# Seven products in another order: the three without a weight sum first

## The chip, the cores and the metric

The kernel runs on one core of one Trainium2 chip. The metric is the device time of one execution in microseconds (us). The reference gives two layers of a decoder trunk for 256 tokens of width 2048, in float32; every large matrix is read from memory once per execution.

## The reference, cut to what matters

```python
for layer in range(2):
    h = rms_norm(x, norm_mix[layer])
    x = x + mixer[layer](h)                  # layer 0: window attention + SSD, layer 1: dilated attention
    h = rms_norm(x, norm_ffn[layer])
    u = jnp.einsum('bsd,df->bsf', h, w_up)   # (256, 2048) x (2048, 8192)
    x = x + jnp.einsum('bsf,fd->bsd', jnp.square(jax.nn.relu(u)), w_down)   # (256, 8192) x (8192, 2048)
```

The change touches the last of these products alone, in both layers: the squared activations times `w_down`.

## The kernel before, in words

**Precision.** Every float32 matrix is split into a high part (a rounded float32r copy, written by ScalarE, `whi`) and a low part (the rest, written by VectorE, `wlo`). A product is three matmuls on TensorE: high by high, high by low, low by high. So each 128x1024 piece of weights (two k-tiles of 128 rows, 512 columns) costs one ScalarE copy (`high`, L314), one VectorE subtraction (`low`, L324) and its matmuls.

**The plan.** All matmul work is one list, `plan`, of pieces; `run` (L291) goes through it. At piece i it issues, in this order, the low part of piece i+2, the load of piece i+6, the high part of piece i+3 and the weight sum of piece i+4 (L353 to L357). Then follow the evictions of the piece before (`pending`, L358), then some steps of the side work (`tick`, L171: transposes, squares, splits of activations), then the matmuls of piece i. Each engine works through its own queue in the order of issue, and semaphores make it wait for the others. There are five `whi` and four `wlo` buffers (L320, L327) and four for freshly loaded weights, `wraw` (L303): a low part can't be written before TensorE is done with the piece four places ahead of it, and a load of such weights waits for the low part that last read its buffer.

**Units and sevens.** An ordinary unit (`Unit`) is one stripe of 512 columns; its pieces have 12 matmuls each and accumulate in two banks (`acc`). `Seven` (L243) instead multiplies 256 tokens by a 1024x1024 block of `w_down` with seven block products in place of eight. It cuts the tokens, the rows and the columns of the block in two. Weights W11, W12, W21, W22 (rows, columns) and linear combinations of them meet activations or their combinations; products are added in PSUM banks (`sp`) and taken from there into the residual stream `res` by VectorE (`evict`, L281). A product is two pieces, h = 0 and 1, of six matmuls each. The raw weights lie in `sraw` tiles: SyncE loads 12 and 11 with product P1, 21 and 22 with P2 (`fetch`, L257). GpSimd adds W22 into tile 12 and then W12 into tile 11 by accumulating DMAs (`accumulate`, L271). Two more sums are made by VectorE (`add`, L265). In the order before:

| product | bank | weights | made from | evicted into (token half, stripe) |
|---|---|---|---|---|
| P1 | a | tile 11 | loaded | (0,0) |
| P2 | b | tile 21 | loaded | (0,0) |
| Q7 | c | tile 12 | accumulated by DMA | (1,1) |
| Q6 | a | tile t2 | 11 + 22, VectorE | (1,0) |
| Q5 | a | tile 11 | accumulated by DMA | (1,1) |
| Q4 | c | tile 21 | 21 + t2, VectorE | (1,0) |
| Q3 | a | tile 22 | loaded | (0,1) |

A bank is not cleared between its products: Q6 adds onto P1, Q5 onto both, and so on. So Q5's first matmul waits until VectorE has read Q6's state of bank a, and Q3's until it has read Q5's.

**Where the sevens stand.** The MLP (`mlp`, L951) has eight chunks c of 1024 hidden columns. In the plan, the products of chunk c stand among the up projections of the chunks after it (`mixed`, L1062): for c = 0 to 5 two sevens per chunk, one after the other, called the first and the second here, and one for c = 6; 13 per layer, 26 in all. For c = 0, 3 and 4, with 19 up pieces, the plan alternates one up piece and two pieces of *different* products, so that Q6's second piece and Q5's first stand side by side. For c = 1 and 2, with 18, it alternates one up piece and the two pieces of *one* product. For c = 5 the spacing is wider, and its second seven ends with six pieces in a row. The last, c = 6, has one piece between two others throughout. Before a chunk's first seven stand five up pieces, and the splits and sums of the next activations fall there.

Of the kernel before, what the change touches and what calls it, by code (L numbers as in the profile page):

```python
# [11 lines left out]
OP = mybir.AluOpType  # L12
# [28 lines left out]
def trunk(ctx: ExitStack, tc: tile.TileContext, x, norm_mix, norm_ffn, w_up, w_down, ab_w_in, ab_q_norm,  # L41
# [33 lines left out]
    V, S, PE = Engine(nc.vector, "V", 90, 1.04), Engine(nc.scalar, "S", 240, 0.83), Engine(nc.tensor, "PE", 0, 0.84)  # L75
# [157 lines left out]
    def unit(*a, **k):  # L233
# [1 line left out]

    SEVEN = (("P1", "a", "11"), ("P2", "b", "21"), ("Q7", "c", "12"), ("Q6", "a", "t2"), ("Q5", "a", "11"),
             ("Q4", "c", "21"), ("Q3", "a", "22"))
    LOADS = {"P1": ("12", "11"), "P2": ("21", "22")}  # L240
    SUMS = {"Q6": ("t2", "11", "22"), "Q4": ("21", "21", "t2")}

    class Seven:  # L243

# [12 lines left out]
        def fetch(self, p, h):  # L257
            for b in LOADS.get(SEVEN[p][0], ()):
                r, c = self.rows[int(b[0]) - 1] + h * KC, self.c0 + (int(b[1]) - 1) * W
                nc.sync.dma_start(self.tile(b, h),  # L260
                                  self.w[r * 128:(r + KC) * 128, c:c + W].rearrange("(k p) c -> p k c", p=128))
                if b == "12":
                    self.accumulate("12", 1, h)

        def add(self, p, h):  # L265
            if SEVEN[p][0] in SUMS:
                o, x, y = SUMS[SEVEN[p][0]]
                x, y = self.raw[x, h], self.raw[y, h]
                V.tensor_tensor(self.raw[o, h] if o != "t2" else self.tile(o, h), x, y, op=OP.add)

        def accumulate(self, b, half, h):  # L271

# [5 lines left out]
        def source(self, p, h):  # L278
            return self.raw[SEVEN[p][2], h]

        def evict(self, p):  # L281

            name, b, _ = SEVEN[p]
            t, j, op = {"P1": (0, 0, OP.add), "P2": (0, 0, OP.add), "Q6": (1, 0, OP.add), "Q7": (1, 1, OP.subtract),
                        "Q5": (1, 1, OP.subtract), "Q4": (1, 0, OP.add), "Q3": (0, 1, OP.subtract)}[name]
            r = self.to[t][j]
            V.tensor_tensor(r, r, self.bank[b], op=op)
            if p == 6 and self.after is not None:
                self.after()

    def run():  # L291
# [60 lines left out]
        for i, (u, c) in enumerate(todo):  # L352
            if i:  # L353
                low(i + AHEAD - 1)
                fetch(i + AHEAD - 1 + RAW)
                high(i + AHEAD)
                add(i + AHEAD + 1)  # L357
# [4 lines left out]
            if isinstance(u, Seven):  # L362
                p, h = c
                name, b, _ = SEVEN[p]
                if p in u.needs and h == 0:
# [836 lines left out]
```

## Time and profile before

| | |
|---|---|
| time, median of three runs | 2342.51 us (2342.3, 2342.51, 2350.98) |
| the profiled execution's own time | 2346.71 us |
| its span, first to last instruction | 2344.9 us |
| TensorE (PE) busy | 2275.7 us, 97% |
| VectorE (DVE) busy | 1771.5 us, 76% |
| ScalarE (ACT) busy | 1296.5 us, 55% |
| mean granted TensorE clock | 0.99 of full speed |
| DMA | 204 GB/s over the span |

The profile is of one execution. Its time is 1.8 us more than its span, and 4.2 us more than the median of the three runs. The sevens run from about 546 us on in layer 0 and from about 1677 to 2325 us in layer 1. A time stands for the whole kernel, but TensorE's idle time lies in a few places; what one of them is worth is read from a window around it.

### The profile page before, as it was taken

The numbers are of one execution on the slowest core, as the hardware profiler recorded it, in microseconds if no ns is written. First come the engines' busy times: TensorE is split into PE (matmuls) and PEld (weight loads), VectorE is DVE, ScalarE is ACT, GpSimd is POOL, SyncE is SP. The second block draws the span as 40 slices with busy tenths as digits, with TensorE's granted clock in tenths as the row PEclk, the third lists the DMA queues.
The fourth block names the chain that finished last, engine by engine and source line by source line (L and its number), as shares of the span: only waits on it lengthen the run. The fifth ranks groups of instructions, "written<-read, shape, count | busy, mean of one in ns | idle before, by whom it ended". The sixth has DMA issues, their size and how long they took to land.

```text
span 2344.9 us, 30293 instructions
## 1 busy us (share of the span) xinstructions
PE 2275.7 (97%) x11005; PEld 1878.8 (80%) x11005; DVE 1771.5 (76%) x2508; ACT 1296.5 (55%) x1627; POOL 133.7 (6%) x124
## 2 busy tenths in 40 slices
PE   8999999999999999999999999999999999999999
PEld 7999988887877878778788778778877877778777
DVE  6779886557877978778976767755687887878796
ACT  5565545445555656556665555554555555556563
POOL 1000000001100011101000000000101101011100
PEclk9999999999999999999999999999999999999999
DMA  7546555569687796978656555446869787696984
GB/s 229 163 136 195 182 175 185 188 186 298 167 256 207 207 288 183 262 206 251 193 172 188 160 155 176 155 161 188 261 172 286 198 241 229 184 295 172 266 229 133
DMA packets 257783, 479.29 MB, mean 204 GB/s; under 512 B 17317, under 2 KB 28113, under 8 KB 257633
## 3 DMA queue, kind: packets, MB, share of 16 engines
q1 hardware_dynamic: 219264, 416.34, 54.2%
q0 software_dynamic: 28800, 54.68, 13.0%
q10 hardware_dynamic: 9568, 6.34, 0.9%
q8 instruction: 86, 1.41, 0.2%
q14 instruction: 65, 0.52, 0.1%
HBM read 475.17 MB, written 2.13 MB: 204 GB/s over the span
## 4 chain that ended last, share of the span: by engine, by line
PE 81%; DMA 13%; DVE 4%; ACT 2%; issue 1%; SPq 0%; ACTq 0%; DVEq 0%
PE acc L71 58%; PE sp L71 17%; DMA wraw<-in_w_up_dram 11%; DVE wlo L71 2%; ACT whi L71 1%; PE uT L71 1%; PE sc L71 1%; PE o L71 1%; PE pT L71 1%; DVE sraw L71 1%; DVE res L71 1%; PE yp L71 1%; PE xT L71 1%; DMA sraw<-in_w_down_dram 1%; DMA wraw<-in_ab_w_in_dram 0%
## 5 line engine op out<-in xcount | busy, mean ns | idle before, releaser
L71 DVE TENSOR_TENSOR wlo<-wraw,whi 128x1024 fp32r<-128x1024 f32 (+1 forms) x584 | 706.6, 1215 | 268.9 <-PE acc L71 158.3
L71 ACT ACTIVATE whi<-wraw 128x1024 fp32r<-128x1024 f32 (+1 forms) x584 | 614.6, 1054 | 505.2 <-PE acc L71 295.3
L71 PE MATMUL acc<-whi,hThi 128*128 128x512 f32 (+1 forms) x1632 | 654.2, 401 | 10.7 <-ACT whi L71 8.5
L71 PE MATMUL acc<-wlo,hThi 128*128 128x512 f32 (+1 forms) x1632 | 641.0, 393 | 7.8 <-DVE wlo L71 7.8
L71 PE MATMUL acc<-whi,hTlo 128*128 128x512 f32 (+1 forms) x1632 | 639.2, 392 | 0.8 <-DVE hTlo L71 0.8
L71 ACT ACTIVATE whi<-sraw 128x1024 fp32r<-128x1024 f32 x364 | 383.6, 1059 | 351.8 <-DVE sraw L71 131.4
L71 DVE TENSOR_TENSOR wlo<-sraw,whi 128x1024 fp32r<-128x1024 f32 x364 | 443.7, 1222 | 131.2 <-ACT whi L71 50.6
L71 PEld LDWEIGHTS acc<-whi,hThi 128*128 128x128 f32 x1632 | 310.8, 190 | 78.7 <-ACT whi L71 10.8
L71 PEld LDWEIGHTS acc<-wlo,hThi 128*128 128x128 f32 x1632 | 310.9, 191 | 74.4 <-DVE wlo L71 14.0
L71 PEld LDWEIGHTS acc<-whi,hTlo 128*128 128x128 f32 x1632 | 310.3, 190 | 66.5 <-DVE hTlo L71 1.7
L274 POOL DMA_DIRECT2D sraw<-in_w_down_dram x104 | 125.3, 1211 | 2130.0 <-DMA sraw<-in_w_down_dram 760.0
L71 PE MATMUL sp<-whi,sh 128*128 128x512 f32 x416 | 164.0, 394 | 23.9 <-DVE res L71 23.9
L71 PE MATMUL sp<-wlo,sh 128*128 128x512 f32 x416 | 163.8, 394 | 0.3
L71 PE MATMUL sp<-whi,sl 128*128 128x512 f32 x416 | 163.8, 394 | 0.0
L71 DVE TENSOR_TENSOR res<-res,sp 128x512 f32<-128x512 f32 x182 | 124.6, 685 | 25.7 <-PE sp L71 25.1
L71 DVE TENSOR_TENSOR sraw<-sraw 128x1024 f32<-128x1024 f32 x104 | 126.9, 1220 | 0.0
L71 PEld LDWEIGHTS sp<-whi,sh 128*128 128x128 f32 x416 | 78.8, 189 | 45.5 <-ACT whi L71 24.7
L71 PE MATMUL acc<-hThi,whi 128*128 128x256 f32 x384 | 112.4, 293 | 0.0
L71 PE MATMUL acc<-hThi,wlo 128*128 128x256 f32 x384 | 108.6, 283 | 0.0
L71 PE MATMUL acc<-hTlo,whi 128*128 128x256 f32 x384 | 108.6, 283 | 0.0
L71 PEld LDWEIGHTS sp<-wlo,sh 128*128 128x128 f32 x416 | 78.6, 189 | 18.0 <-DVE wlo L71 2.2
L71 PEld LDWEIGHTS sp<-whi,sl 128*128 128x128 f32 x416 | 78.8, 189 | 16.4
(227 smaller groups left out, 2781.0 us busy)
## 6 DMA issues: line engine op xcount, KB each, us to landing
wraw<-in_w_up_dram SPq DMA_DIRECT2D x256, 512.0 KB, 5.0
sraw<-in_w_down_dram SPq DMA_DIRECT2D x208, 512.0 KB, 9.4
sraw<-in_w_down_dram POOLq DMA_DIRECT2D x104, 512.0 KB, 9.8
wraw<-in_ab_w_in_dram SPq DMA_DIRECT2D x96, 512.0 KB, 3.6
wraw<-in_c_w_qkv_dram SPq DMA_DIRECT2D x96, 512.0 KB, 4.1
wraw<-in_ab_w_out_dram SPq DMA_DIRECT2D x48, 512.0 KB, 3.5
wraw<-in_w_down_dram SPq DMA_DIRECT2D x48, 512.0 KB, 4.0
wraw<-in_c_w_o_dram SPq DMA_DIRECT2D x32, 512.0 KB, 3.5
```

The costliest lines, as they stand in the source:

```text
L71: return f(out, *a, **k)
L274: nc.gpsimd.dma_start(self.raw[b, h], self.w[r * 128:(r + KC) * 128, c:c + W].rearrange("(k p) c -> p k c", p=128), accum_op=OP.add)
```

## The change

The order of the seven products becomes P1, P2, Q3, Q7, Q6, Q5, Q4. Q3 gets a bank `d` of its own, which holds Q3 alone. Since bank a no longer passes through Q3, output (0,1) is made of two evictions: Q3's from d, and a second one of Q5's bank a. So VectorE has eight evictions per seven in place of seven, 26 more in all. The sum for Q6 is written over tile 22, which Q3 has used by then, and Q4 adds this tile; the tile t2 is no longer allocated (two per seven). The number of sums, of loads and of matmuls stays, and so does the order of the queues of SyncE, GpSimd and ScalarE.

```diff
@@ -235,10 +235,10 @@
 
 
 
-    SEVEN = (("P1", "a", "11"), ("P2", "b", "21"), ("Q7", "c", "12"), ("Q6", "a", "t2"), ("Q5", "a", "11"),
-             ("Q4", "c", "21"), ("Q3", "a", "22"))
+    SEVEN = (("P1", "a", "11"), ("P2", "b", "21"), ("Q3", "d", "22"), ("Q7", "c", "12"), ("Q6", "a", "22"),
+             ("Q5", "a", "11"), ("Q4", "c", "21"))
     LOADS = {"P1": ("12", "11"), "P2": ("21", "22")}
-    SUMS = {"Q6": ("t2", "11", "22"), "Q4": ("21", "21", "t2")}
+    SUMS = {"Q6": ("22", "11", "22"), "Q4": ("21", "21", "22")}
 
     class Seven:
 
@@ -266,7 +266,7 @@
             if SEVEN[p][0] in SUMS:
                 o, x, y = SUMS[SEVEN[p][0]]
                 x, y = self.raw[x, h], self.raw[y, h]
-                V.tensor_tensor(self.raw[o, h] if o != "t2" else self.tile(o, h), x, y, op=OP.add)
+                V.tensor_tensor(self.raw[o, h], x, y, op=OP.add)
 
         def accumulate(self, b, half, h):
 
@@ -281,10 +281,11 @@
         def evict(self, p):
 
             name, b, _ = SEVEN[p]
-            t, j, op = {"P1": (0, 0, OP.add), "P2": (0, 0, OP.add), "Q6": (1, 0, OP.add), "Q7": (1, 1, OP.subtract),
-                        "Q5": (1, 1, OP.subtract), "Q4": (1, 0, OP.add), "Q3": (0, 1, OP.subtract)}[name]
-            r = self.to[t][j]
-            V.tensor_tensor(r, r, self.bank[b], op=op)
+            for t, j, op in {"P1": ((0, 0, OP.add),), "P2": ((0, 0, OP.add),), "Q6": ((1, 0, OP.add),),
+                             "Q7": ((1, 1, OP.subtract),), "Q4": ((1, 0, OP.add),), "Q3": ((0, 1, OP.subtract),),
+                             "Q5": ((1, 1, OP.subtract), (0, 1, OP.subtract))}[name]:
+                r = self.to[t][j]
+                V.tensor_tensor(r, r, self.bank[b], op=op)
             if p == 6 and self.after is not None:
                 self.after()
```

**First place: VectorE's queue in the first seven of chunk 0, layer 0.** `wlo_...<-wraw` is the low part of an up piece, `wlo_...<-sraw` that of a seven's piece, `sraw<-sraw` a weight sum, `res<-res,sp` an eviction. Before, from the low part of the up piece behind the third product's first piece on:

```order
L71 TENSOR_TENSOR wlo_5443<-wraw_5379,whi_5429 128x1024
L71 TENSOR_TENSOR sraw_5447<-sraw_5220,sraw_5294 128x1024
L71 TENSOR_TENSOR wlo_5455<-sraw_5264,whi_5445 128x1024
L71 TENSOR_TENSOR res_82<-res_82,sp_5418 128x512
L71 TENSOR_TENSOR wlo_5467<-sraw_5447,whi_5457 128x1024
L71 TENSOR_TENSOR sraw_5473<-sraw_5267,sraw_5343 128x1024
L71 TENSOR_TENSOR wlo_5487<-wraw_5427,whi_5471 128x1024
L71 TENSOR_TENSOR wlo_5497<-sraw_5473,whi_5489 128x1024
L71 TENSOR_TENSOR res_82<-res_82,sp_5460 128x512
L71 TENSOR_TENSOR wlo_5508<-sraw_5220,whi_5499 128x1024
```

The same stretch in the changed kernel:

```order
L71 TENSOR_TENSOR wlo_5443<-wraw_5379,whi_5429 128x1024
L71 TENSOR_TENSOR wlo_5453<-sraw_5343,whi_5445 128x1024
L71 TENSOR_TENSOR res_82<-res_82,sp_5418 128x512
L71 TENSOR_TENSOR wlo_5465<-sraw_5217,whi_5455 128x1024
L71 TENSOR_TENSOR wlo_5483<-wraw_5427,whi_5469 128x1024
L71 TENSOR_TENSOR sraw_5294<-sraw_5220,sraw_5294 128x1024
L71 TENSOR_TENSOR wlo_5494<-sraw_5264,whi_5485 128x1024
L71 TENSOR_TENSOR res_82<-res_82,sp_5458 128x512
L71 TENSOR_TENSOR wlo_5506<-sraw_5294,whi_5496 128x1024
L71 TENSOR_TENSOR sraw_5343<-sraw_5267,sraw_5343 128x1024
L71 TENSOR_TENSOR wlo_5530<-wraw_5467,whi_5510 128x1024
L71 TENSOR_TENSOR wlo_5540<-sraw_5343,whi_5532 128x1024
```

The two sums for Q6 stand one product later, behind the low part of another up piece; a further eviction (Q3's, `sp_5458`) stands between; and `sraw_5294`, which is tile 22, takes the sum in place of the new tile `sraw_5447`.

**Second place: VectorE's queue at the end of the second seven of chunk 2.** Before, the low part of Q3's last piece, the eviction of Q4, the low parts of the first up pieces before the next chunk's sevens, and Q3's eviction:

```order
L71 TENSOR_TENSOR wlo_8180<-sraw_7917,whi_8172 128x1024
L71 TENSOR_TENSOR res_82<-res_82,sp_8015 128x512
L71 TENSOR_TENSOR wlo_8193<-wraw_8134,whi_8184 128x1024
L71 TENSOR_TENSOR wlo_8218<-wraw_8147,whi_8197 128x1024
L71 TENSOR_TENSOR wlo_8233<-wraw_8170,whi_8225 128x1024
L71 TENSOR_TENSOR res_82<-res_82,sp_7933 128x512
```

In the changed kernel:

```order
L71 TENSOR_TENSOR wlo_8179<-sraw_7915,whi_8171 128x1024
L71 TENSOR_TENSOR res_82<-res_82,sp_7933 128x512 x2
L71 TENSOR_TENSOR wlo_8193<-wraw_8132,whi_8183 128x1024
L71 TENSOR_TENSOR wlo_8218<-wraw_8145,whi_8197 128x1024
L71 TENSOR_TENSOR wlo_8233<-wraw_8169,whi_8225 128x1024
L71 TENSOR_TENSOR res_82<-res_82,sp_8054 128x512
```

Here the low part is that of Q4's last piece, the eviction of Q5 stands twice, and the low parts of the up pieces come behind both.

**Third place: VectorE's queue in the last six pieces of the second seven of chunk 5.** Before, from the eviction of Q6 on:

```order
L71 TENSOR_TENSOR res_82<-res_82,sp_9489 128x512
L71 TENSOR_TENSOR wlo_9664<-sraw_9419,whi_9648 128x1024
L71 TENSOR_TENSOR wlo_9676<-sraw_9460,whi_9668 128x1024
L71 TENSOR_TENSOR wlo_9688<-sraw_9421,whi_9680 128x1024
L71 TENSOR_TENSOR res_82<-res_82,sp_9489 128x512
L71 TENSOR_TENSOR wlo_9704<-sraw_9462,whi_9695 128x1024
L71 TENSOR_TENSOR wlo_9716<-wraw_9666,whi_9708 128x1024
L71 TENSOR_TENSOR res_82<-res_82,sp_9573 128x512
```

In the changed kernel, from the eviction of Q7 on:

```order
L71 TENSOR_TENSOR res_82<-res_82,sp_9610 128x512
L71 TENSOR_TENSOR wlo_9661<-sraw_9366,whi_9646 128x1024
L71 TENSOR_TENSOR sraw_9419<-sraw_9419,sraw_9421 128x1024
L71 TENSOR_TENSOR wlo_9674<-sraw_9393,whi_9665 128x1024
L71 TENSOR_TENSOR sraw_9460<-sraw_9460,sraw_9462 128x1024
L71 TENSOR_TENSOR wlo_9687<-sraw_9419,whi_9678 128x1024
L71 TENSOR_TENSOR res_82<-res_82,sp_9489 128x512
L71 TENSOR_TENSOR wlo_9703<-sraw_9460,whi_9694 128x1024
L71 TENSOR_TENSOR wlo_9715<-wraw_9663,whi_9707 128x1024
L71 TENSOR_TENSOR res_82<-res_82,sp_9489 128x512 x2
```

Before, the six pieces in a row are those of Q5, Q4 and Q3, and both sums stand ahead of them. Now they are those of Q6, Q5 and Q4, and the sums for Q4 stand between the low parts, ahead of Q6's eviction (the first `sp_9489` row).

## Rows read from the trace of the kernel before

**Rows 1.** The page, part 1: busy us (share of the span) xinstructions
```profile
PE 2275.7 (97%) x11005; PEld 1878.8 (80%) x11005; DVE 1771.5 (76%) x2508; ACT 1296.5 (55%) x1627; POOL 133.7 (6%) x124
```
**Rows 2.** Waits of PE, whole span: us in total, times, longest us
```profile
PE sp L71 <- DVE res L71: 23.9, 14, 3.0
```
**Rows 3.** Timeline, PE, first seven: start us, us, engine line operation [idle before <-releaser]
```profile
567.80 0.39 PE L71 MATMUL sp<-whi,sh 128*128 128x512 f32 x1
...
568.93 0.39 PE L71 MATMUL sp<-whi,sl 128*128 128x512 f32 x1
...
572.28 0.47 PE L71 MATMUL sp<-whi,sh 128*128 128x512 f32 x1 [2.96 <-DVE res L71]
```
**Rows 4.** Windows, busy us by engine: six of 3.0 us behind Q6, summed
```profile
sum 18.00, PE 0.82 PEld 0.94 DVE 18.00 ACT 11.22 POOL 0.87; mean PE 0.14 PEld 0.16 DVE 3.00 ACT 1.87 POOL 0.15
```
**Rows 5.** Timeline, PE, second seven of the same chunk
```profile
614.06 0.47 PE L71 MATMUL sp<-whi,sh 128*128 128x512 f32 x1 [0.87 <-DVE res L71]
```
**Rows 6.** Timeline, DVE, first seven of chunk 0
```profile
557.59 1.23 DVE L71 TENSOR_TENSOR wlo<-wraw,whi 128x1024 fp32r<-128x1024 f32 x1 [0.53 <-ACT whi L71]
...
566.31 0.68 DVE L71 TENSOR_TENSOR res<-res,sp 128x512 f32<-128x512 f32 x1
566.91 1.22 DVE L71 TENSOR_TENSOR wlo<-sraw,whi 128x1024 fp32r<-128x1024 f32 x1
568.04 1.22 DVE L71 TENSOR_TENSOR wlo<-wraw,whi 128x1024 fp32r<-128x1024 f32 x1
...
571.45 0.68 DVE L71 TENSOR_TENSOR res<-res,sp 128x512 f32<-128x512 f32 x1
```
**Rows 7.** Groups, DVE, 557.6 to 571.4 us: busy us, mean ns | idle before
```profile
L71 DVE TENSOR_TENSOR wlo<-sraw,whi 128x1024 fp32r<-128x1024 f32 x5 | 6.1, 1220 | 0.1
L71 DVE TENSOR_TENSOR wlo<-wraw,whi 128x1024 fp32r<-128x1024 f32 x3 | 3.7, 1221 | 0.5 <-ACT whi L71 0.5
L71 DVE TENSOR_TENSOR sraw<-sraw 128x1024 f32<-128x1024 f32 x3 | 3.7, 1220 | 0.0
L71 DVE TENSOR_TENSOR res<-res,sp 128x512 f32<-128x512 f32 x2 | 1.4, 682 | 0.0
```
**Rows 8.** Windows: us; PE, PEld, DVE, ACT, POOL busy (count); PEclk; DMA share; GB/s
```profile
572.70:576.00 3.30, 3.30 (x12) 2.62 (x11) 2.93 (x3) 0.24 (x1) 1.19 (x1) 0.50 1.05 407
576.00:579.40 3.40, 3.40 (x16) 2.81 (x15) 0.82 (x1) 1.93 (x3) 0.00 (x0) 0.99 1.07 357
867.70:871.10 3.40, 3.40 (x15) 2.85 (x16) 3.22 (x3) 2.42 (x4) 1.20 (x1) 1.00 1.07 333
```
**Rows 9.** Timeline, DVE and PE, end of the second seven of chunk 5
```profile
1117.82 0.69 DVE L71 TENSOR_TENSOR res<-res,sp 128x512 f32<-128x512 f32 x1 [0.29 <-PE sp L71]
...
1124.16 1.22 DVE L71 TENSOR_TENSOR ul<-uf,uh 128x1024 fp32r<-128x1024 f32 x1
1125.43 0.50 PE L71 MATMUL acc<-whi,ul 128*128 128x512 f32 x1 [0.75 <-DVE ul L71]
```
**Rows 10.** Timeline, DVE and SyncE's queue (SPq), end of chunk 0
```profile
625.73 0.69 DVE L71 TENSOR_TENSOR res<-res,sp 128x512 f32<-128x512 f32 x1 [0.30 <-PE sp L71]
626.34 2.36 DVE L71 TENSOR_TENSOR wlo<-wraw,whi 128x1024 fp32r<-128x1024 f32 x2
627.58 0.37 SPq L306 DMA_DIRECT2D wraw<-in_w_up_dram  x1
628.13 2.16 SPq L260 DMA_DIRECT2D sraw<-in_w_down_dram  x4
```
**Rows 11.** Waits of ACT, 640 to 660 us, start of the next chunk's sevens
```profile
ACT whi L71 <- DMA sraw<-in_w_down_dram: 9.6, 2, 6.9
```
**Rows 12.** Windows, ten at the starts of first sevens, P2 to Q7: one, and the sum
```profile
849.00:855.00 6.00, 4.40 (x16) 2.74 (x16) 4.57 (x5) 2.51 (x3) 0.00 (x0) 1.00 0.87 327
...
sum 60.50, PE 33.66 PEld 20.92 DVE 27.86 ACT 23.38 POOL 0.00; mean PE 3.37 PEld 2.09 DVE 2.79 ACT 2.34 POOL 0.00
```
**Rows 13.** Timeline, PE, P2's first matmul, on a bank just taken
```profile
551.86 0.39 PE L71 MATMUL sp<-whi,uh 128*128 128x512 f32 x1
```

## The prediction

> **What bounds the kernel now.** I read the page's busy shares first, then the waits of TensorE, then timelines where those waits are. TensorE is busy 97% of the span and VectorE 76% [rows 1], so VectorE's extra work costs nothing as such; it counts where TensorE waits for VectorE. TensorE's own waits name one such place: `sp` matmuls waited 23.9 us for `res`, in 14 waits of at most 3.0 us [rows 2]. `res` is written by the evictions, so the question is which eviction.
>
> It is Q6's. In chunk 0 TensorE begins Q6's second piece at 567.80, its sixth matmul at 568.93, and Q5's first matmul at 572.28, after 2.96 us of nothing [rows 3]. Q5 adds onto bank a and waits until Q6's state is read out. The same stands in the first seven of chunks 0, 3 and 4 of both layers: six windows of 3.0 us hold 0.82 us of TensorE work together, 17.2 us idle, while VectorE is busy in all 18.00 [rows 4]. In the second sevens of these chunks the wait is 0.87 us [rows 5], six times 5.2. The two other waits of the 14 are the rest, 23.9 - 17.2 - 5.2 = 1.5.
>
> Why 2.96 here and 0.87 there? 0.87 is what remains when VectorE is ready: from TensorE's end to the eviction and back. In the first seven VectorE is late. From 557.59 it works without a pause until Q6's eviction starts at 571.45 [rows 6]: 13.9 us, in which stand 8 low parts, 3 sums and 2 evictions with 0.1 us idle inside [rows 7]. From start to start a 1024-column operation takes 568.04 - 566.91 = 1.13 us and an eviction 566.91 - 566.31 = 0.60 [rows 6]; 11 x 1.13 + 2 x 0.60 = 13.6, which fits. TensorE needs 1.13 us for five matmuls [rows 3], 0.227 each: 1.36 for a seven's piece, 2.72 for an up piece. One up piece and two seven's pieces are 5.44; VectorE's three low parts and one eviction for them are 4.0. Without sums VectorE gains 1.4 on TensorE in each such turn, with one sum 0.3. It starts late, because the first seven's loads and the next activations' splits come late, and Q6's eviction comes before it has caught up.
>
> **The change part by part.**
> *Sums one product later.* They now stand behind one more turn without a sum (first place of the order). Up to Q6's eviction VectorE has 11 low parts, 3 sums and 3 evictions, 4.0 us more; TensorE has 5.44 more. The lateness falls by 1.4 us in each of six first sevens. The stalls, 17.2 / 6 = 2.87 on average, become about 1.4: -6 x 1.44 = **-8.6 us**. From both sides: -6 x (2.87 - 0.87) = -12.0 if VectorE catches up wholly, 0 if what is added eats the gain. I take the count of the queue, since VectorE is shown to run without pause here. Q6 and Q5 still share bank a, so 0.87 stays in all twelve.
>
> *The clock after those stalls.* Behind the first, TensorE's granted clock is 0.50 for the next 3.3 us, that is 1.2 in place of 2.4 GHz, and 0.99 again after that; behind the second stall, at 867.7, it stays at 1.00 [rows 8]. By the same view four of the six have such a fall (chunks 0 and 4 of both layers). Each costs half of about 3.4 us, 1.7. Stalls of half the length should bring fewer; no 0.87 stall has one behind it. I take two fewer: **-3.4**; bounds -6.8 and, if shorter ones do the same, 0.
>
> *The end of chunk 5.* Its second seven ends in six pieces without an up piece between. Before, these are Q5, Q4, Q3, an up piece stands between Q6 and Q5, and VectorE is on time: Q5's eviction at 1117.82 had to wait for TensorE [rows 9]. Now they are Q6, Q5, Q4 (third place). Between Q7's eviction and Q6's, VectorE has three low parts and two sums, 5.65 us. Counted from TensorE's end of Q7: 0.2 until its eviction starts, 0.6 for it, 5.65, so Q6's starts at 6.45. TensorE has one up piece and Q6 until then, 2.72 + 2.72 = 5.44. VectorE is 1.0 late, and the stall is 1.0 + 0.87 = 1.9. Behind it comes the split `ul`, for which TensorE waits already [rows 9]; the second eviction of Q5 and the pushed queue move it by another 0.4. Twice (both layers) 2.3: **+4.6**; bounds 2 x 0.87 = +1.7 and, with a fall of the clock behind each, +8.0.
>
> *The first sevens of chunk 5.* Q6's second piece and Q5's first now stand side by side here too: 2 x 0.87 = 1.7, against the 1.5 of the two other waits: **+0.2**.
>
> *One eviction more.* 26 x 0.60 = 15.6 us of VectorE. Beside TensorE's matmuls it is hidden, but for one place: at a chunk's end (second place) the low part of the first up piece stands right behind it. The load of up weights that waits for this low part, and SyncE's queue behind it, hold the next chunk's `sraw` loads. In chunk 0 the eviction starts at 625.73, the low part at 626.34, the load is issued at 627.58 when it ends, the four `sraw` loads at 628.13 [rows 10]. All of it moves by 0.6. These loads are what TensorE starves for: ScalarE waited 9.6 us in two waits for them [rows 11], and at the ten starts that follow another chunk, windows of 60.50 us hold 33.66 of TensorE, 27 idle [rows 12]. So 10 x 0.6 = **+6.0**; bounds +6.0 and 0, if the burst ends when its bytes are through. I take the upper one, since TensorE waits on landings there.
>
> *At no cost.* Q3's bank: a first matmul on a bank just taken starts without a wait [rows 13], and its tenant before has been read a turn earlier; if not, 0.87 per seven, 23 at most. The tile t2: loads find free tiles sooner, but wait at chunk ends for the up weights, not for tiles. Tile 22 is needed earlier, by Q3 in place of Q6's sum; it is loaded right behind tile 21, which is needed sooner still. The sums in place have the same shape. SyncE's, GpSimd's and ScalarE's queues are unchanged.
>
> Sum: -8.6 - 3.4 + 4.6 + 0.2 + 6.0 = -1.2 us. Against the profiled execution, 2346.7, that is 2345.5; that execution was 4.2 above the median of the runs, so I forecast **2341.3**.
>
> A rule against this change stands in the Trainium skill, "TensorE: Matmul & The Clock Gate", section "A second HAM failure mode: psum-queue depth-cycling": a matmul stream that goes through PSUM banks in turn idles briefly between its groups, and the clock falls and rises with it. By it a fourth bank would add falls at 26 starts of Q3, 26 x 1.7 = 44 us. The start on a fresh bank shows no idle time [rows 13], and the fall of rows 8 stands behind an idle stretch of almost 3 us, so by the trace it would add none.
>
> **The rivals.**
> *A, the forecast:* VectorE's lateness falls and the longer queue at chunk ends gives it back: 2341.3; with the terms' spread 2336 to 2346. 50%.
> *B, faster:* the late loads are hidden, since the burst ends when its bytes are through (0 in place of +6.0), and none of the six stalls has a fall behind it (-6.8): -8.6 - 6.8 + 4.6 + 0.2 = -10.6, 2332. With the chunk-end price at its lower bound, 2329. For it: the shorter stalls are near those that had no fall. Against: the loads are issued the moment the low part ends. 22%.
> *C, slower:* the starts of the chunks decide. Four of the ten starts (chunks 3 and 4 of layer 0, 3 and 5 of layer 1) have no fall now, as the window of 6.00 us with 4.40 of work and a clock of 1.00 [rows 12]. If 0.6 more of idle time tips them, and the two chunk ends fall too, that is 6 x 1.7 = 10.2; with no fall saved at Q6: -8.6 + 4.6 + 0.2 + 6.0 + 10.2 = +12.4, 2355. It decides from three new falls on. For it: the six other starts have one, with more idle time before it. Against: 0.6 is little beside the 1.6 idle in that window. 12%.
> *D, the change doesn't take the wait away:* Q6 and Q5 keep their bank, and if VectorE's gained turn is eaten by the side work that shifts into it, the stalls stay: 0 in place of -8.6 and -3.4, +10.8, 2353. Against: no split stands in the listed queue. 14%.
> *E, the skill's rule:* new falls at each Q3; 2380 and more. 2%.
>
> **How the numbers follow.** What a measurement of this kernel can tell from no change is about 0.5%, 11.7 us: below 2330.8 is faster, above 2354.2 slower. Faster is the lower half of B, 11%. Slower is two thirds of C, over a quarter of D, and E, 14%; the rest is the same, 75%. The range leaves out a tenth on each side: 2331 to 2354; A's own is 2336 to 2346.
>
> **What would show it.** Right: in the first sevens of chunks 0, 3, 4 the wait for `res` before Q5 is about 1.4 us (1.2 to 2.0), in the second 0.87; two new waits of about 1.9 stand at the ends of chunk 5; the `sraw` loads at chunk ends are issued 0.6 later after the double eviction, and TensorE idles about 33 in place of 27 us in the ten start windows. Wrong: waits of 2.9 remain (D), idle time at the starts unchanged (B), or 0.50 in stretches that read 1.00 now (C), or waits at Q3's first matmul (E).

## The result: slower by 0.4%, and the profile after

The changed kernel takes 2353.52 us (median of ten runs, 2351.61 to 2356.37), the kernel before on the same chip 2343.61 (2341.07 to 2350.98). The ratio is 1.0041, 95% interval 1.0031 to 1.0051: 9.9 us slower, where 1.2 faster was forecast. The profiled executions took 2346.71 and 2353.53 us, 6.8 apart; the one of before was 3.1 above its median, the one after at it.

First the page's busy line of the changed kernel, against [rows 1]. VectorE's added evictions show (26 more instructions, 13.5 us); the shares are the same:

```profile
PE 2279.3 (97%) x11005; PEld 1882.3 (80%) x11005; DVE 1785.0 (76%) x2534; ACT 1294.3 (55%) x1627; POOL 133.8 (6%) x124
```

TensorE's waits after (us in total, times, longest us):

```profile
PE sp L71 <- DVE res L71: 22.4, 16, 2.4
...
PE acc L71 <- DVE ul L71: 2.4, 2, 1.2
```

The wait that the change works on has hardly shrunk, 22.4 for 23.9 [rows 2]: it has moved. The timeline of TensorE shows Q5's first matmul in the first seven of chunk 0 and of chunk 3 (start, length, operation, idle before in brackets):

```profile
575.40 0.47 PE L71 MATMUL sp<-whi,sh 128*128 128x512 f32 x1 [0.87 <-DVE res L71]
...
871.35 0.47 PE L71 MATMUL sp<-whi,sh 128*128 128x512 f32 x1 [2.38 <-DVE res L71]
```

In chunk 0 of both layers it is down to 0.87 us, what remains when VectorE is ready (2.96 in layer 0 before [rows 3]); in chunks 3 and 4 it is still 1.9 to 2.4. The six together fell from 17.2 to 10.8 us, by 6.4 where 8.6 was forecast. Here are VectorE's first low part and Q6's eviction in chunk 3:

```profile
852.66 1.23 DVE L71 TENSOR_TENSOR wlo<-wraw,whi 128x1024 fp32r<-128x1024 f32 x1 [1.82 <-ACT whi L71]
...
870.52 0.68 DVE L71 TENSOR_TENSOR res<-res,sp 128x512 f32<-128x512 f32 x1
```

VectorE does not pause between them. The 17.9 us are 4.0 more than the 13.9 before, as the queue had been counted. But VectorE's first low part itself moved against TensorE. In chunk 3 TensorE ends Q6 16.3 us behind it (11.7 before), so TensorE's share grew by 4.6 us and not by 5.44, and the wait shrank by 0.6; in chunk 0 it is 17.9 (11.7 before), 6.1 more, and the wait shrank by 2.1. Why the start moved so is not shown.

At the end of chunk 5 a new wait stands. VectorE there, from Q7's eviction to Q6's:

```profile
1111.36 0.68 DVE L71 TENSOR_TENSOR res<-res,sp 128x512 f32<-128x512 f32 x1
1111.96 1.22 DVE L71 TENSOR_TENSOR wlo<-sraw,whi 128x1024 fp32r<-128x1024 f32 x1
1113.10 1.22 DVE L71 TENSOR_TENSOR sraw<-sraw 128x1024 f32<-128x1024 f32 x1
1114.23 1.22 DVE L71 TENSOR_TENSOR wlo<-sraw,whi 128x1024 fp32r<-128x1024 f32 x1
1115.36 1.22 DVE L71 TENSOR_TENSOR sraw<-sraw 128x1024 f32<-128x1024 f32 x1
1116.50 1.22 DVE L71 TENSOR_TENSOR wlo<-sraw,whi 128x1024 fp32r<-128x1024 f32 x1
1117.63 0.68 DVE L71 TENSOR_TENSOR res<-res,sp 128x512 f32<-128x512 f32 x1
```

It doesn't pause. The timeline of TensorE has Q7's last matmul first. TensorE then ends Q6, waits, and goes on at half its rate (0.43 us from matmul to matmul in place of 0.23). Later it waits for the split `ul`:

```profile
1110.32 0.39 PE L71 MATMUL sp<-whi,sl 128*128 128x512 f32 x1
...
1115.76 0.39 PE L71 MATMUL sp<-whi,sl 128*128 128x512 f32 x1
1118.47 0.69 PE L71 MATMUL sp<-whi,sh 128*128 128x512 f32 x1 [2.31 <-DVE res L71]
1118.95 0.63 PE L71 MATMUL sp<-wlo,sh 128*128 128x512 f32 x1
1119.38 0.63 PE L71 MATMUL sp<-whi,sl 128*128 128x512 f32 x1
...
1128.43 0.51 PE L71 MATMUL acc<-whi,ul 128*128 128x512 f32 x1 [1.19 <-DVE ul L71]
```

The windows say why (us; PE, PEld, DVE, ACT, POOL busy; granted clock; DMA share; GB/s): the clock is at 1.2 in place of 2.4 GHz behind each of the two waits, for 3.4 us each time. The same stands at the end of chunk 5 in layer 1. Such a stretch at the lower level is called a fall below.

```profile
1115.00:1118.40 3.40, 1.15 (x6) 0.61 (x4) 3.40 (x5) 2.19 (x3) 1.20 (x1) 1.00 0.40 66
1118.60:1122.00 3.40, 3.40 (x9) 2.64 (x10) 1.90 (x2) 0.73 (x2) 0.00 (x0) 0.51 0.76 135
1122.00:1125.40 3.40, 3.40 (x17) 2.78 (x15) 2.50 (x4) 2.44 (x3) 0.00 (x0) 1.00 0.52 140
1128.80:1132.20 3.40, 3.40 (x10) 2.64 (x9) 3.40 (x4) 1.64 (x2) 0.00 (x0) 0.50 1.05 352
```

At the end of chunk 0, VectorE's timeline after, against [rows 10]:

```profile
621.32 1.29 DVE L71 TENSOR_TENSOR res<-res,sp 128x512 f32<-128x512 f32 x2 [0.29 <-PE sp L71]
622.52 2.36 DVE L71 TENSOR_TENSOR wlo<-wraw,whi 128x1024 fp32r<-128x1024 f32 x2
```

The loads in SyncE's queue (SPq):

```profile
624.19 2.38 SPq L260 DMA_DIRECT2D sraw<-in_w_down_dram  x4
```

From the first eviction's start to the low part it is now 1.20 us, 0.61 before, and the loads follow 1.67 behind that (1.79 before), so they come 0.5 us later where 0.6 was forecast. For what it costs, I took ten windows of 15 us from the first matmul of P2 on, at the starts that follow another chunk. The row of chunk 3 in layer 0 and the sum, before:

```profile
844.10:859.10 15.00, 13.40 (x53) 9.41 (x52) 10.30 (x10) 6.96 (x8) 0.00 (x0) 1.00 0.95 303
...
sum 150.00, PE 121.73 PEld 88.32 DVE 94.79 ACT 77.57 POOL 0.00; mean PE 12.17 PEld 8.83 DVE 9.48 ACT 7.76 POOL 0.00
```

After, the same start and the sum:

```profile
841.30:856.30 15.00, 12.07 (x42) 8.66 (x41) 7.82 (x8) 8.27 (x9) 0.00 (x0) 0.89 0.88 264
...
sum 150.00, PE 116.34 PEld 82.97 DVE 85.51 ACT 86.01 POOL 0.00; mean PE 11.63 PEld 8.30 DVE 8.55 ACT 8.60 POOL 0.00
```

TensorE's idle time there is 150 - 121.73 = 28.3 us before and 33.7 after: 5.4 more, 6.0 forecast. A clock of 0.89 over 15 us is 1.7 us lost; summed so over the ten windows, 15.1 were lost before and 16.9 after. Over the whole profile TensorE's busy time, which grows when its clock is low, rose by 3.6 us (2275.7 to 2279.3), and its idle time by 3.2 (69.2 to 72.4).

Place by place, from the first matmul of a seven to that of the next, the profiled pair differs so:

| place | forecast us | measured us |
|---|---|---|
| first sevens of chunks 0, 3, 4 (six) | -8.6 - 3.4 + 2.4 = -9.6 | -8.8 |
| first sevens of chunks 1, 2 (four) | +2.4 | +4.0 |
| first sevens of chunk 5 (two) | +0.2 + 1.2 = +1.4 | -0.8 |
| second sevens of chunk 5 (two) | +4.6 | +12.4 |
| the twelve other sevens, and the rest | 0 | 0.0 |
| sum | -1.2 | +6.8 |

(The 6.0 of the starts is spread at 0.6 a start.) One row is far off: 6.2 us at each end of chunk 5.

### The profile page after: what moved, and what is told of

Same layout as the page of the kernel before. It is cut to its first block, busy times and chain, and to the rows that moved or that the text cites. A ratio compares the mean times of both kernels' runs of the same rounds, so it can differ in the third digit from the quotient of the medians.

```text
span 2351.7 us, 30275 instructions
## 1 busy us (share of the span) xinstructions
PE 2279.3 (97%) x11005; PEld 1882.3 (80%) x11005; DVE 1785.0 (76%) x2534; ACT 1294.3 (55%) x1627; POOL 133.8 (6%) x124
## 4 chain that ended last, share of the span: by engine, by line
PE 82%; DMA 12%; DVE 4%; ACT 1%; issue 1%; SPq 0%; ACTq 0%; DVEq 0%
PE acc L71 59%; PE sp L71 17%; DMA sraw<-in_w_down_dram 6%; DMA wraw<-in_w_up_dram 5%; DVE wlo L71 2%; PE uT L71 1%; PE sc L71 1%; DVE res L71 1%; PE o L71 1%; ACT whi L71 1%; PE pT L71 1%; PE yp L71 1%; DMA wraw<-in_ab_w_in_dram 1%; PE xT L71 0%; DVE sraw L71 0%
## 5 line engine op out<-in xcount | busy, mean ns | idle before, releaser
L71 PEld LDWEIGHTS acc<-whi,hThi 128*128 128x128 f32 x1632 | 310.7, 190 | 81.1 <-ACT whi L71 13.9
L71 PE MATMUL sp<-whi,sh 128*128 128x512 f32 x416 | 165.0, 397 | 22.4 <-DVE res L71 22.4
L71 DVE TENSOR_TENSOR res<-res,sp 128x512 f32<-128x512 f32 x208 | 140.2, 684 | 25.5 <-PE sp L71 24.2
L71 PEld LDWEIGHTS sp<-whi,sh 128*128 128x128 f32 x416 | 79.0, 190 | 44.8 <-ACT whi L71 23.7
```

The lines of the kernel that those rows point to most:

```text
L71: return f(out, *a, **k)
```

## The experiments

Three theories. **T1**: the loss is made at the ends of chunk 5, by six pieces in a row with Q6 beside Q5 and the sums between; the first sevens gain about as forecast; the starts give some of it back. **T2**: the extra eviction in each of 26 sevens costs. **T3**: falls of the clock come and go with any shift of the program. A mixed kernel gives each `Seven` its order by name, "old" or "new", with that order's sums and evictions. Each kernel was timed beside the kernel before on its own chip, and differences are against that. Where two of these kernels are set against each other, it is by these differences.

**The order before at the two ends alone.**

```diff
-                         marks[c][-1], (lambda: sevens_end(j)) if c == NC - 2 else None).pieces
+                         marks[c][-1], (lambda: sevens_end(j)) if c == NC - 2 else None,
+                         "old" if c == NC - 3 and j == 2 else "new").pieces
```

> The changed kernel, but the second seven of chunk 5 of both layers runs in the order before (two sevens of 26). T1 (the loss is made at the ends of chunk 5: between the two profiles these two sevens grew by 6.2 and 6.3 us): about 12 us below the changed kernel, 2341, so about 2 us below the kernel before; the falls of the clock behind these ends are gone. T2 (the loss is VectorE's extra eviction, spread over all 26 sevens): two evictions fewer of 26, at most 1 us below the changed kernel, about 2353. T3 (falls of the clock that come and go with any shift of the program): the ends change little in sum, since falls come up elsewhere; 2347 to 2356.

Measured: 2343.9 us, ratio 0.9993 (0.9984 to 1.0003), 1.2 below the kernel before, so 11 less than the whole change. Both sevens take 40.6 us as before, and the wait for `ul` is back at

```profile
1123.61 0.50 PE L71 MATMUL acc<-whi,ul 128*128 128x512 f32 x1 [0.74 <-DVE ul L71]
```

T2 is out as the main cause. But what is gained without the ends is 1.2 us, where the other terms of the prediction make 5.8: something else costs more than forecast.

**The new order at the two ends alone.**

```diff
+                         "new" if c == NC - 3 and j == 2 else "old").pieces
```

> The kernel before, but the second seven of chunk 5 of both layers runs in the new order, all others as before. T1: the whole loss and more, about 12 us above the kernel before (2355 to 2356), with a stall of about 2.3 us before Q5 and two falls of the clock at each end. T2: two evictions more of 26, under 1 us above the kernel before, 2344. T3: within 4 us of the kernel before, either side.

Measured: 2354.49 us, ratio 1.0042 (1.0029 to 1.0055), +9.4 (6.8 to 12.9 by the interval). Two sevens of 26 alone cost as much as the whole change. The wait and the windows behind it are those of the changed kernel:

```profile
1118.94 0.77 PE L71 MATMUL sp<-whi,sh 128*128 128x512 f32 x1 [2.31 <-DVE res L71]
...
1128.83 0.66 PE L71 MATMUL acc<-whi,ul 128*128 128x512 f32 x1 [1.16 <-DVE ul L71]
```

Its windows:

```profile
1118.80:1122.20 3.40, 3.26 (x8) 2.61 (x9) 1.82 (x2) 0.65 (x2) 0.00 (x0) 0.50 0.88 142
1129.00:1132.40 3.40, 3.40 (x9) 2.66 (x10) 3.39 (x3) 1.87 (x2) 0.00 (x0) 0.50 1.02 342
```

**The new order in six first sevens alone.**

```diff
+                         "new" if c in (0, 3, 4) and j == 0 else "old").pieces
```

> The kernel before, but the first sevens of chunks 0, 3 and 4 of both layers (six of 26) run in the new order; every chunk end stays as before. T1: only the gain stays, the 8.6 us of shorter stalls before Q5 and up to 3.4 us of falls that don't come: 2332 to 2335. T2: the gain is small beside six evictions more, 2340 to 2344. T3: gains and falls in any order, 2338 to 2348.

Measured: 2333.07 us, ratio 0.9950 (0.9937 to 0.9962), -12.0 (9 to 15 by the interval), the sum of the two gain terms of the prediction. That it fits so closely is in part luck. The stalls are as in the changed kernel (0.87 in chunk 0, 2.3 and 2.4 in chunks 3 and 4), 11.3 us together, so they gave 5.9 and not 8.6; two of them have a fall behind, four before, the 3.4 us of the forecast. The stall in chunk 4 of layer 0 and the fall behind it:

```profile
965.53 0.47 PE L71 MATMUL sp<-whi,sh 128*128 128x512 f32 x1 [2.42 <-DVE res L71]
```

```profile
967.00:970.40 3.40, 3.40 (x10) 2.62 (x9) 1.79 (x2) 1.06 (x1) 0.00 (x0) 0.51 1.06 373
```

The remaining 2.7 us of the 12.0 are not assigned to a place here.

**The second eviction one piece later**, in the changed kernel: behind the low part of the next up piece.

```diff
-            pending = []
+            pending, later = later, []
...
                     pending.append(lambda u=u, p=p: u.evict(p))
+                    if name == "Q5":
+                        later.append(lambda u=u, p=p: u.evict(p, True))
```

> The changed kernel, but the second eviction of Q5's bank is issued one piece later, so that at a chunk's end the low part of the next up piece no longer stands behind two evictions. The term of the prediction for it (ten starts by 0.6 us): 6 us below the changed kernel, 2347 to 2348, with TensorE's idle time at the ten starts 6 us less. T1: the starts of chunks 1 and 2 cost 3.9 us more in the profile after and the wait for the split at the ends of chunk 5 0.45 us each, so 0 to 5 us below the changed kernel; the stalls before Q5 and the falls behind the ends of chunk 5 stay. T2: nothing, 2353, since the number of evictions is the same.

Measured: 2347.01 us, ratio 1.0009 (1.0000 to 1.0018), +1.9, so 8 less than the whole change. TensorE's idle time in the ten windows is 29.6 us (33.7 without the delay), 4.1 less where 6 was expected. Part of the 8 us is something else: the ends of chunk 5 took 45.2 us in place of 46.8, with the same wait and one fall fewer:

```profile
1114.86 0.47 PE L71 MATMUL sp<-whi,sh 128*128 128x512 f32 x1 [2.31 <-DVE res L71]
...
1123.24 0.53 PE L71 MATMUL acc<-whi,ul 128*128 128x512 f32 x1 [1.19 <-DVE ul L71]
```

The windows behind the two waits:

```profile
1114.00:1117.40 3.40, 2.54 (x11) 2.14 (x12) 2.91 (x4) 1.93 (x3) 0.00 (x0) 1.00 0.90 143
...
1123.60:1127.00 3.40, 3.40 (x10) 2.63 (x9) 3.40 (x4) 1.66 (x2) 0.00 (x0) 0.50 0.99 337
```

**Both edits: the old order at the ends, the rest late.**

> The changed kernel with both edits of the first two single tests: the second seven of chunk 5 in the order before, and the second eviction of Q5's bank one piece later everywhere else. T1 (ends of chunk 5, and beside them the starts behind a double eviction): the ends give 9.2 us (two sevens of 45.2 us in the late kernel, 40.6 in the order before), so 2347.0 - 9.2 = 2338. T3 (falls come up elsewhere): 2342 to 2347.

Measured: 2337.32 us, ratio 0.9970 (0.9958 to 0.9982), -7.5, as T1 had it.

**The new order in ten second sevens alone** (chunks 0 to 4), which leaves the double evictions ahead of the ten starts and neither the gain nor the ends.

```diff
+                         "new" if c < NC - 3 and j == 2 else "old").pieces
```

> The kernel before, but the second sevens of chunks 0 to 4 of both layers (ten of 26, those that end ahead of another chunk's start) run in the new order. No stall of a first seven is touched, and no end of chunk 5: what is left is the double eviction ahead of ten starts. The term of the prediction for it (0.6 us each): 6 us above the kernel before, 2351. If only the falls at the starts count (T3): between -4 and +10. If the burst of loads ends when its bytes are through: 0, 2345.

Measured: 2353.55 us, ratio 1.0038 (1.0026 to 1.0050), +8.8. The ten windows:

```profile
sum 150.00, PE 117.39 PEld 83.64 DVE 88.05 ACT 77.45 POOL 0.00; mean PE 11.74 PEld 8.36 DVE 8.81 ACT 7.74 POOL 0.00
```

**The same with the second eviction one piece later.**

> The kernel before it (new order in the second sevens of chunks 0 to 4 alone), with the second eviction of Q5's bank one piece later, so that the low part of the next up piece stands behind one eviction as in the kernel before. If the place of the second eviction is what counts: within 1.5 us of the kernel before, 2345. If the order itself or the eviction anywhere counts: as far above it as the test without the delay, 2350.

Measured: 2347.5 us, ratio 1.0011 (1.0002 to 1.0020), +2.7, where at most 1.5 was expected: 6 of the 8.8 hang on the place of that one instruction. At the end of chunk 0, without the delay, the evictions, the low parts and the next chunk's loads are

```profile
624.25 1.29 DVE L71 TENSOR_TENSOR res<-res,sp 128x512 f32<-128x512 f32 x2 [0.29 <-PE sp L71]
625.45 2.36 DVE L71 TENSOR_TENSOR wlo<-wraw,whi 128x1024 fp32r<-128x1024 f32 x2
...
627.11 2.24 SPq L267 DMA_DIRECT2D sraw<-in_w_down_dram  x4
```

and with it

```profile
624.34 0.69 DVE L71 TENSOR_TENSOR res<-res,sp 128x512 f32<-128x512 f32 x1 [0.29 <-PE sp L71]
624.95 1.22 DVE L71 TENSOR_TENSOR wlo<-wraw,whi 128x1024 fp32r<-128x1024 f32 x1
...
626.61 2.28 SPq L267 DMA_DIRECT2D sraw<-in_w_down_dram  x4
```

The loads come 2.27 us behind the first eviction's start in place of 2.86. The idle time is 29.8 in place of 32.6:

```profile
sum 150.00, PE 120.23 PEld 85.92 DVE 94.28 ACT 78.01 POOL 0.00; mean PE 12.02 PEld 8.59 DVE 9.43 ACT 7.80 POOL 0.00
```

That is 2.8 us less; the ten windows lost 10.1 us to the clock in place of 20.1. In this pair the clock counts for more than the idle time. The mean granted clock over all runs rises with the delay in each of the three pairs of kernels that have it: 0.9884 to 0.9914 here, 0.9881 to 0.9906 in the changed kernel, 0.9906 to 0.9922 with the old order at the ends.

Over all profiles: where two evictions stand ahead of the low part at chunk ends (four kernels) the ten windows hold 32.6 to 34.4 us of idle time and lose 13.6 to 20.4 to the clock; in the ten others 27.7 to 30.7 and 8.5 to 15.1. The kernel before's profiled execution, with 15.1, is the worst of these ten.

**Chunk 5 spread evenly**, the changed kernel and the kernel before, so that no six pieces stand in a row.

```diff
-                mixed(x, seven(c, 0) + seven(c, 2), 4.5, n + (3 if c == NC - 3 else 0))
+                mixed(x, seven(c, 0) + seven(c, 2), 4.5, n)
```

> The changed kernel with chunk 5's sevens spread evenly over its up pieces (spacing as in chunks 3 and 4), so that its second seven no longer ends with six pieces in a row; no product's order is touched. T1 (no up piece between Q6 and Q5, and both sums between, makes the end's loss): the stall before Q5 at the two ends falls from 2.28 to 0.87 us and no fall of the clock stands behind it; the two first sevens of chunk 5 then have stalls as in chunks 3 and 4, 2.4 us in place of 0.84. Against the kernel before with the same spacing: 8.6 x 8/6 + 3.4 = 15 us gained in the eight first sevens, 6 to 9 lost at ten starts, so 6 to 9 us below it. T2 or T3: 5 to 10 us above it, as the changed kernel stands to the kernel before.

> The kernel before with chunk 5's sevens spread evenly, the other side of the comparison. T1: two more stalls of 2.9 us, in the first sevens of chunk 5, and two of 0.87 in the second, with a fall behind some: 5 to 10 us above the kernel before, and 6 to 9 above the changed kernel with the same spacing. T2 or T3: 5 to 10 us below that one.

Measured: 2348.45 us with the new order (ratio 1.0011, 1.0002 to 1.0020), 2353.67 with the old (1.0036, 1.0022 to 1.0049). With the row of six gone the change is 5.2 us *faster*, by the same order of products; 6 to 9 was expected. The second sevens of chunk 5 take 47.9 us in both kernels, where they took 46.8 and 40.6 with the row of six. In the new order the end's wait, and the window behind it, are

```profile
1112.67 0.47 PE L71 MATMUL sp<-whi,sh 128*128 128x512 f32 x1 [0.87 <-DVE res L71]
```

```profile
1112.70:1116.10 3.40, 3.40 (x15) 2.83 (x16) 3.23 (x3) 1.31 (x2) 0.00 (x0) 1.00 0.85 142
```

No fall stands there. So it isn't the new order at that place that costs, but the new order without up pieces between.

**Q6 ahead of Q7, and the late eviction**, so that Q7 stands between Q6 and Q5 on bank a.

```diff
-    SEVEN = (("P1", "a", "11"), ("P2", "b", "21"), ("Q3", "d", "22"), ("Q7", "c", "12"), ("Q6", "a", "22"),
+    SEVEN = (("P1", "a", "11"), ("P2", "b", "21"), ("Q3", "d", "22"), ("Q6", "a", "22"), ("Q7", "c", "12"),
```

> The changed kernel with Q6 ahead of Q7 (order P1, P2, Q3, Q6, Q7, Q5, Q4), so that Q7 stands between Q6 and Q5 on bank a, and with the second eviction of Q5 one piece later. T1: the 23 us that matmuls wait for res go, down to 2 at most, and with them five falls of 1.7 us (behind the stalls of the first sevens and at the ends of chunk 5): 2347.0 - 21 - 8 = 2318, 2315 to 2325. T3: the waits go, falls come up elsewhere: 2326 to 2330.

Measured: 2320.38 us, ratio 0.9897 (0.9884 to 0.9910), -24.4. No wait for `res` is left. The ends still cost 44.8 and 43.5 us: VectorE's lateness now meets the split. VectorE works without a pause from 1093.38 until `ul` is written, and TensorE waits for that:

```profile
1110.13 0.80 PE L71 MATMUL acc<-whi,ul 128*128 128x512 f32 x1 [2.26 <-DVE ul L71]
```

**The same, with the old order at the two ends.**

> The order with Q7 between Q6 and Q5 and the late second eviction, but the second seven of chunk 5 of both layers in the order before. In the kernel with the swapped order everywhere these two sevens took 44.8 and 43.5 us, since the wait moved from Q5 to the split behind the seven (2.2 us each) with a fall of the clock; in the order before they take 40.6. T1: 7 us below it, 2313. T3: falls come up elsewhere, 2317 to 2320.

Measured: 2316.18 us, ratio 0.9870 (0.9850 to 0.9890), -28.2: 4 below the last one, 7 expected. In the profiles the ends gave 6.0 (40.6 and 41.7 us), and a new fall in the first seven of chunk 0 took 2.0 back, T3 in small.

**The second eviction two pieces later.**

```diff
-            pending, later = later, []
+            pending, later, latest = later, latest, []
```

> The same kernel with the second eviction of Q5's bank two pieces later in place of one, so that the low part of the second up piece at a chunk's end no longer stands behind it either. If each load of the next chunk waits on the low part ahead of it and TensorE on the loads (the price of 0.6 us a start): up to 6 us below the kernel with one piece of delay, 2307. If the first low part alone decides, or the burst of loads ends when its bytes are through: the same time, 2313.

Measured: 2315.01 us, ratio 0.9866 (0.9845 to 0.9887), which can't be told from the last one. These two are 1.3% faster than the kernel before, and by the ratios 1.7% faster than the changed kernel.

## Why the prediction was wrong

**The step that failed** is "The end of chunk 5", sized at +4.6; the two ends grew by 12.4 us, and alone they cost 9.4. Its mechanism was right: the queue was read as three low parts and two sums ahead of Q6's eviction, and that is what stands there. Two things were too small. The wait is 2.3 us in place of 1.9, since VectorE was already late at Q7's eviction: it starts at 1111.36, 0.65 us after Q7's last matmul ended at 1110.71, where the prediction took 0.2. A VectorE that is ready takes less still. In the kernel before, an eviction follows the last matmul, which ends at 613.19, at once:

```profile
612.80 0.39 PE L71 MATMUL sp<-whi,sl 128*128 128x512 f32 x1
613.23 0.69 DVE L71 TENSOR_TENSOR res<-res,sp 128x512 f32<-128x512 f32 x1 [0.21 <-PE sp L71]
```

The 0.21 there is VectorE's idle time, and from TensorE's end to its start it is 0.04. With that, the prediction's own working gives 1.7, and 0.6 of lateness makes the 2.3.

And the clock was taken at nothing, with one fall per end as the outer bound; there are two per end, behind Q5's wait and behind `ul`'s, 1.7 us each: 2.3 + 0.45 more at `ul` + 3.4 = 6.2 per end. A wait of 1.9 lay between one that often had a fall behind it and one that never had, and the sum priced it like the shorter one.

**One eviction more**, +6.0: right in its mechanism (load behind low part behind second eviction), and the idle time of the changed kernel's ten windows, +5.4, is near it. But moving the eviction takes back only 2.8 to 4.1 us of idle time in the three pairs, so the rest of it has another source, and the term left out the clock: alone it costs 8.8, with 20.1 us lost to the clock in the ten windows, 15.1 in the kernel before. That the longer idle time brings these falls is likely, not shown. Of rival C the half on the chunk ends came true, with two falls each where it named one. Of its four starts without a fall only one had one in the profile after, chunk 3 of layer 0 (0.89 in the row of 841.30, 1.00 before).

**Sums one product later**, -8.6, and **the clock after those stalls**, -3.4: right in mechanism and in sum, -12.0 alone. The stalls were not "about 1.4": 0.87 in chunk 0, 1.9 to 2.4 in chunks 3 and 4, so they gave 5.9 to 6.4 and not 8.6. Rival D (nothing gained) fell, though its time, 2353, is the one that was measured: the gain came, and was spent elsewhere.

**The first sevens of chunk 5**, forecast at +1.4 with their starts, came out at -0.8. In layer 0 the window at their start has a granted clock of 0.89 before and 1.00 after, so a fall there is gone; this was not tried alone.

**The forecast's last step** took off 4.2 us because the profiled execution of before stood that far above the median. Of these, 1.1 are the median of three runs against that of ten (2342.51 and 2343.61), and 3.1 are that the changed kernel's profiled execution stood at its median and not above it: the median moved by 9.9 where the profiles differ by 6.8. A likely reason is the clock. That execution of before lost more to it at the starts than any other profile without the double eviction, and the changed kernel has a low clock in all its runs: 0.986 to 0.990, 0.988 on average, where the kernel before's runs on the four chips of the experiments average 0.991 to 0.992. Over 2350 us that difference is 7 to 9 us; it is an upper bound, since TensorE also waits within falls. So most of the 9.9 us can be clock, which the forecast had only in one term, as a gain. Of the miss of 12.2 us the ends are 7.8; this step is most of the rest.

Rival E fell: a fourth bank adds no idle time. TensorE passes from P2 to Q3's fresh bank in the first seven of chunk 0 without a gap:

```profile
557.35 0.39 PE L71 MATMUL sp<-whi,ul 128*128 128x512 f32 x1
557.58 0.39 PE L71 MATMUL sp<-whi,sh 128*128 128x512 f32 x1
```

The whole profile has 12 stretches at the low level, 55.6 us together, where it had 11 with 45.2: not 26 more. So the rule of the Trainium skill, "TensorE: Matmul & The Clock Gate", section "A second HAM failure mode: psum-queue depth-cycling", does not describe this stream of matmuls; by it the change would have cost some 44 us.

The tests by parts, -12.0, +8.8 and +9.4, add up to +6.2 beside the whole's +9.9; each is known to about 3 us. What the first sevens of chunks 1, 2 and 5 and chunk 6 add was not measured alone.

## What to carry to other kernels

A reordering is priced place by place: where filler work stands between two dependent pieces it may gain, and the same order loses where the filler runs out; it can be used at the one place and not at the other. A wait on a matmul engine can cost its length and the clock behind it, so for a wait between one that had a fall and one that hadn't, take the fall into the sum and not only into the bounds. An extra instruction on an engine with time to spare can still cost when the next load's release is queued behind it: try it one step later.

## What the runs showed of the hardware

The length of a wait alone doesn't settle whether the clock falls. Behind the same 2.31 us, at the same place of the program, the granted clock was 0.51 in the changed kernel and 1.00 in the one with the late eviction; what decides it is left open here. In the last kernel a fall stands even behind a wait of 0.89, which follows one of 0.74 by 1.6 us:

```profile
1107.32 0.58 PE L71 MATMUL acc<-whi,ul 128*128 128x512 f32 x1 [0.89 <-DVE ul L71]
```

```profile
1107.60:1111.00 3.40, 3.40 (x9) 2.64 (x9) 3.23 (x3) 2.03 (x3) 0.00 (x0) 0.50 1.01 355
```

So the prediction's reading that no wait of 0.87 has a fall behind it holds for the profile before, and not as a rule. And when Q7 took the wait for `res` away, the lateness did not go: VectorE had the same work to do by the end of the row of six, and the next reader of its results, `ul`, waited 2.26 in place of 1.19 us.
